# Block products for all input projections, and half of the output projection moved beside attention

## The chip, the core and the metric

The kernel runs on one core of a Trainium2 chip. TensorE (PE) multiplies matrices and adds up in 8 banks of PSUM; VectorE (DVE), ScalarE (ACT) and GpSimd (POOL) work element by element; SyncE (SP) issues DMA transfers between DRAM and the on-chip memory. Each engine runs its own instructions in their order and waits on semaphores for the others. The metric is the device time of one execution in microseconds; less is better.

## The reference

One layer of a decoder, 1024 tokens by 1024 features, all in f32:

```
h    = x @ w_in                # columns: pool 512 | q 512 | k 512 | v 512 | forget gate 8
pool = scale * GroupLinear(trailing_mean(u, win) - u)     # 4 groups of 128, win 2, 4, 8, 16
c    = cumsum(log_sigmoid(gate + b_f))                    # per head, 8 heads of 64
attn = softmax(q k' / 8 + c_t - c_s, causal) @ v
x    = layer_norm(alpha * x + concat(pool, attn) @ w_out)
x    = layer_norm(alpha * x + relu(x @ w_mlp1)**2 @ w_mlp2)   # hidden width 4096
```

## The kernel before

**Precision.** Each f32 operand is split into a rounded high part and the rest (`split`: a copy on ScalarE, L71, and a subtraction on VectorE, L72). A product is three matmuls: high by high, high by low, low by high (`three`, L83 to L85). So each 128-deep step of a product is three matmuls into a PSUM bank.

**Stages, in the order of time.**

1. Values and gate (L161 to L164): the 512 value columns and 8 gate columns, 260 in a matmul, for 8 tiles of 128 tokens by two halves by 8 depth steps by 3: 384 matmuls. The values (`V`) and all of x as high and low parts (`xs`, 8 blocks of the tag "B") stay on chip. Five blocks of the output weights are split meanwhile and put into DRAM (`split_output_weights`, L201).
2. Pool groups 3, 2 and 1 (`pool_group`), and keys and queries of head pair 0 (`qk_proj`): columns of 128 by two halves of 512 tokens by 8 depth steps by 3, 48 matmuls a column. The pooled differences pass through a small linear step (`pool_linear`) and into `mix_dram`.
3. Attention, head pairs 0 to 3. A unit is one head and 256 query rows. `att_probs` makes scores on PE (L370, L371), adds the gate row and finds the row maximum in one VectorE operation (L376), and exponentiates on ScalarE (L378). `att_values`, for the unit before, transposes the probabilities (L398), splits them (L399, L400) and multiplies by the values (L414). `fillstep` puts projection matmuls between them: keys and queries of the next pair, and pool group 0 during the last pair. The gate row of a head is 1024 sums of logarithms, spread to 128 partitions by a transfer from `ncf_dram` (L347); the first POOL or VectorE operation on a score needs it.
4. Output projection (from L771): per 128-token tile two halves of 512 columns, each 8 depth blocks by 3 matmuls (4 pooled, 4 from attention); then alpha * x added (L809), the norm on VectorE (`Norm.on_vector`), and the tile transposed for the MLP (`x1_transposed`).
5. The MLP, from 412 us to the end, already in seven block products of half size (`product`, L627, and combinations).

**What sets the order.** The program is written in the order in which each engine is to work; a scheduler keeps this order on each engine. Buffers are slots of a tag with a fixed count (14 "B" slots of 1 MB, 10 "Q", 9 "A" of half that); a transfer into a slot waits until the slot's last readers are done. All loads named here are issued by SP, one after the other: one that waits for its slot holds up all behind it. POOL issues some stores.

Of the kernel before, what the change touches and what calls it, by code (L numbers as in the profile page):

```python
# [32 lines left out]
EARLY, LATE = (3, 2, 1), (0,)  # L33
# [3 lines left out]
def trunk(ctx, tc, xT, xn, wuqk, wvf, bf, poolw, pscale, wout, g1, b1, w1, w2, g2, b2, out):  # L37
# [10 lines left out]
    NBUF = {"S": 3, "U": 2, "B": 14, "Q": 10, "A": 9}  # L48
    uid = [0]

    def slot(tag, shape, dt=F32R):
        uid[0] += 1
        return sb.tile([P] + list(shape), dt, tag=tag, bufs=NBUF[tag], name=f"{tag}{uid[0]}")

# [18 lines left out]

    def load_w(src):
        st = slot("S", [KT, P], F32)
        nc.sync.dma_start(st, src)
        w = slot("B", [2, KT, P])
        split(w[:, 0], w[:, 1], st)
        return w[:, 0], w[:, 1]
# [29 lines left out]
    ASIDE = 3  # L109
    wo_dram = dr.tile([KT - ASIDE, 2, P, D], F32, name="wo_dram")  # L110


    xs = {}

    def load_x(c, kp):
        st = slot("Q", [2, CH], F32)
        x = slot("B", [2, 2, CH])
        if c or kp:
            nc.sync.dma_start(st, xT[c, kp])
        for k in range(2):  # L120
            t = x[:, k]
            xs[c, 2 * kp + k] = t
            first = c == kp == k == 0
            for i, r in enumerate((slice(0, 256), slice(256, CH)) if first else (slice(0, CH),)):
                if c == kp == 0:
                    (nc.scalar if first and i == 0 else nc.sync).dma_start(st[:, k, r], xT[c, kp, :, k, r])
                split(t[:, 0, r], t[:, 1, r], st[:, k, r])
                yield

    wv = []  # L130

    def load_wvf(kp):
        st = slot("S", [2, 2 * VW], F32)
        hi, lo = slot("A", [2, 2 * VW]), slot("A", [2, 2 * VW])
        wv.append((hi, lo))
        if kp:
            nc.sync.dma_start(st, wvf[kp])
        for k in range(2):
            if kp == 0:
                nc.sync.dma_start(st[:, k], wvf[kp, :, k])  # L140
            for c in [slice(0, VW), slice(VW, 2 * VW)] if kp == 0 and k == 0 else [slice(0, 2 * VW)]:
                split(hi[:, k, c], lo[:, k, c], st[:, k, c])
                yield

    V = [None] * NT
    z = small([P, NT, NH], "z")

    def vf_mm(t, half, dst, k):
# [24 lines left out]
    for kp in range(4):  # L173

        gw, gx = load_wvf(kp), load_x(0, kp)
        for g in (gw, gx, gw, gx, gw, gx):
            next(g, None)
# [300 lines left out]
    att_values(*pend)  # L478

# [691 lines left out]
```

## Time and profile before

| | us |
|---|---|
| median of 3 runs | 1040.67 (1040.50 to 1040.82) |
| span of the profiled execution, first to last instruction | 1039.2 |
| values and gate | 5.2 to 53.6 |
| pool groups 3 to 1, pair 0 | 53.6 to 110.3 |
| attention | 110.3 to 322.5 |
| output projection | 323 to 412 |
| MLP | 412 to 1039.2 |

The profiled execution's own time is its span; the median of the runs is 1.5 us above it. The stage borders are the starts of the first matmuls of a stage's lines. Engine rows are read as busy time, instructions in parentheses; a matmul's duration there is longer than the distance to the next one, since they overlap, so the price of a matmul is read from packed stretches and not from its mean.

### The profile page before, as it was taken

The page shows a single profiled execution, that of the slowest core. Times are in us where ns is not written, and L with a number is a line of the kernel's source. Part 1 is how long each engine was busy: PE and PEld are TensorE (multiplying, and loading weights), DVE is VectorE, ACT ScalarE, POOL GpSimd, SP SyncE. Part 2 cuts the span into 40 slices and gives each one's busy share as a digit, 9 for nine tenths or more (in the row PEclk, how much of TensorE's full clock was granted, in tenths as well). Part 3 has the DMA queues.
Part 4 walks back from the last instruction along what each step waited for, and adds up shares of the span by engine and source line. Part 5 has one row for each costly group of instructions (what it writes and reads, how often), then busy time and mean ns, then how long its engine had stood idle before and what let it go on. Part 6 is the DMA issues. An engine that isn't in the chain of part 4 may idle for free.

```text
span 1039.2 us, 14092 instructions
## 1 busy us (share of the span) xinstructions
PE 1016.9 (98%) x4976; PEld 844.9 (81%) x4976; DVE 760.8 (73%) x1303; ACT 510.7 (49%) x820; POOL 142.7 (14%) x246
## 2 busy tenths in 40 slices
PE   9999999999989999999999999999999999999996
PEld 9988888878777888887888888888788888888884
DVE  4776678777786887988878778788875566566547
ACT  4623566666673321676766766768531221122152
POOL 0200112111000021113122122120100000000057
PEclk9999999999999999999999999999999999999998
DMA  9702211111376642139667566566999888878753
GB/s 358 274 27 87 98 52 52 34 50 54 101 250 207 195 148 102 62 134 349 266 240 276 215 262 263 227 231 221 346 308 305 283 264 281 271 228 271 242 186 121
DMA packets 114678, 206.29 MB, mean 199 GB/s; under 512 B 9576, under 2 KB 77992, under 8 KB 114608
## 3 DMA queue, kind: packets, MB, share of 16 engines
q1 hardware_dynamic: 96896, 141.82, 41.1%
q0 software_dynamic: 17280, 62.92, 15.6%
q8 instruction: 39, 0.64, 0.2%
q10 hardware_dynamic: 432, 0.66, 0.2%
q14 instruction: 31, 0.25, 0.1%
HBM read 132.42 MB, written 72.94 MB: 198 GB/s over the span
## 4 chain that ended last, share of the span: by engine, by line
PE 50%; issue 4%; DVE 3%; DMA 1%; POOL 1%; SPq 0%; ACT 0%; DVEq 0%; POOLq 0%
PE s L981 15%; PE pv L981 8%; PE s L627 8%; PE mm L627 6%; PE pt L627 6%; PE pv L627 4%; PE pt L981 2%; PE mm L981 2%; DMA hid_dram<-A 1%; DMA A<-hid_dram 1%; DVE B L72 1%; POOL hid_dram L752 0%; POOL A L620 0%; SPq L960 0%; DVE A L750 0%
## 5 line engine op out<-in xcount | busy, mean ns | idle before, releaser
L71 ACT CAST B<-S 128x1024 fp32r<-128x1024 f32 (+1 forms) x79 | 69.0, 885 | 168.8 <-DMA S<-in_w_dram 61.2
L627 PE MATMUL s<-B,Q 128*128 128x512 f32 x480 | 113.5, 389 | 0.2 <-ACT B L71 0.2
L627 PEld LDWEIGHTS s<-B,Q 128*128 128x128 f32 x480 | 90.0, 188 | 19.3 <-ACT B L71 0.6
L72 DVE TENSOR_TENSOR B<-S,B 128x1024 fp32r<-128x1024 f32 (+1 forms) x79 | 79.4, 1013 | 29.9 <-ACT B L71 29.8
L981 PE MATMUL s<-B,Q 128*128 128x512 f32 x390 | 94.8, 389 | 0.0
L71 ACT CAST Q<-S 128x1024 fp32r<-128x1024 f32 x52 | 54.7, 1052 | 64.0 <-PE s L627 17.0
L981 PEld LDWEIGHTS s<-B,Q 128*128 128x128 f32 x390 | 73.2, 188 | 15.6
L981 PE MATMUL s<-B,A 128*128 128x512 f32 x333 | 83.1, 394 | 1.2 <-DMA A<-hid_dram 1.2
L752 POOL DMA_DIRECT2D hid_dram<-A x90 | 48.3, 542 | 217.1 <-ACT A L749 174.7
L981 PEld LDWEIGHTS s<-B,A 128*128 128x128 f32 x333 | 62.4, 188 | 15.9 <-DMA A<-hid_dram 1.9
L72 DVE TENSOR_TENSOR Q<-S,Q 128x1024 fp32r<-128x1024 f32 x52 | 63.4, 1219 | 15.6 <-ACT Q L71 15.5
L627 PE MATMUL pt<-B,Q 128*128 128x512 f32 x300 | 71.6, 389 | 0.0
L627 PE MATMUL mm<-B,Q 128*128 128x512 f32 x300 | 71.6, 389 | 0.0
L414 PE MATMUL pv<-A,B 128*128 128x256 f32 x320 | 64.0, 299 | 3.0 <-DVE A L400 1.6
L627 PEld LDWEIGHTS mm<-B,Q 128*128 128x128 f32 x300 | 56.3, 188 | 11.7
L627 PEld LDWEIGHTS pt<-B,Q 128*128 128x128 f32 x300 | 56.3, 188 | 11.7
L414 PEld LDWEIGHTS pv<-A,B 128*128 128x128 f32 x320 | 49.6, 188 | 19.0 <-ACT A L399 8.8
L400 DVE TENSOR_TENSOR A<-pt,A 128x512 fp32r<-128x512 f32 (+1 forms) x80 | 49.2, 634 | 18.2 <-ACT A L399 17.7
L378 ACT ACTIVATE A<-A,nm 128x1024 f32<-128x1024 f32 (+7 forms) x64 | 49.8, 778 | 20.0 <-DVE nm L376 19.6
L750 DVE TENSOR_TENSOR A<-A,A 128x1024 f32<-128x1024 f32 x45 | 53.6, 1220 | 0.0
L399 ACT CAST A<-pt 128x512 fp32r<-128x512 f32 (+1 forms) x80 | 41.7, 540 | 18.5 <-PE pt L398 17.3
L981 PE MATMUL pv<-B,Q 128*128 128x512 f32 x204 | 50.3, 390 | 0.0
(407 smaller groups left out, 2309.7 us busy)
## 6 DMA issues: line engine op xcount, KB each, us to landing
hid_dram<-A POOLq DMA_DIRECT2D x105, 512.0 KB, 4.0
S<-in_w_dram SPq DMA_DIRECT2D x62, 512.0 KB, 3.7
Q<-hid_dram SPq DMA_DIRECT2D x101, 256.0 KB, 5.1
A<-hid_dram SPq DMA_DIRECT2D x79, 256.0 KB, 4.5
S<-in_wuqk_dram SPq DMA_DIRECT2D x12, 512.0 KB, 3.3
wo_dram<-Q POOLq DMA_DIRECT2D x10, 512.0 KB, 4.0
B<-wo_dram SPq DMA_DIRECT2D x10, 512.0 KB, 4.1
A<-ncf_dram SPq DMA_DIRECT2D x8, 512.0 KB, 3.9
```

The costliest lines, as they stand in the source:

```text
L71: nc.scalar.copy(hi, src)
L72: nc.vector.tensor_tensor(lo, src, hi.bitcast(F32), ALU.subtract)
L378: nc.scalar.activation(pt[:, :nk], pt[:, :nk], AF.Exp, bias=nm, scale=-1.0, accum_out=rsum[h][:, i : i + 1])
L399: nc.scalar.copy(tt[:, 0, ev], tp[:, ev])
L400: nc.vector.tensor_tensor(tt[:, 1, ev], tp[:, ev], tt[:, 0, ev].bitcast(F32), ALU.subtract)
L414: nc.tensor.matmul(ov, V[j][:, h].rearrange("p s d -> p (s d)"), tt[:, s, a:b], start=(j == 0 and s == 0), stop=(j == 2 * m + 1 and s == 1),)
L627: nc.tensor.matmul(dst, b[x][:, k], A[a][y][:, k], start=first and k == 0 and i == 0, stop=k == H - 1 and i == 2, skip_group_check=not first,)
L750: nc.vector.tensor_tensor(x, x, hi.bitcast(F32), ALU.subtract)
L752: nc.gpsimd.dma_start(hid_dram[self.u, :, i, AT[name] : AT[name] + 2 * CH], part.rearrange("p q n t -> p (q n t)"))
L981: nc.tensor.matmul(dst, h[:, p_], w[q_], start=first and u == self.us[0] and j == 0, stop=u == self.us[-1] and j == 2, skip_group_check=no ...
```

## The change

- **Block products.** With x and the weights cut into halves along both the contracted axis and the output axes, a product of 2x2 blocks is formed from seven block products of sums instead of eight. The values do this with halves of tokens by halves of columns (`v_product`, 7 x 48 = 336 matmuls of 260). Pool groups and keys/queries are taken two columns at a time, in six `Columns` (groups 3 and 2; 1 and 0; key and query of each pair), 7 products of 12 matmuls each: 504 of 512 columns, instead of 576. On chip are now seven blocks of x (A11, A12, A22 and four sums S1 to S4), high and low: all 14 "B" slots. Block sums are made by POOL and VectorE, combinations of products by ScalarE and VectorE.
- **All before attention.** Every projection, all four pool groups too, is finished before attention. Values go to `v_dram`, keys and queries (high and low, `kq_dram`), the pooled mix, already split (`pool_dram`), and all 8 blocks of the split output weights (`wo_dram`) to DRAM. Keys and queries, values and four blocks of the output weights are loaded back into "B" slots as the blocks of x are let go (`load_pair`, `load_values`, `load_output_weights`).
- **Memory in phases.** The "Q" and "A" memory is given anew to each phase ("v", "c", "t", "m": values, columns, attention, rest) with other tags; a new tile waits for the last user of the memory that it covers.
- **Pooled half beside attention.** `fillstep` now runs `pooled_output`: the pooled half of the output projection, 192 matmuls, with alpha * x added, into `xa_dram`.
- **After attention** the output projection has only the attention half (192 matmuls); the tile is read from `xa_dram`; the inverse row sums are multiplied in on POOL; norms of tiles 0 to 5 use `by_three` (ScalarE and four POOL operations, stores by SP) instead of `on_vector`; the transposes come two tiles later instead of one.

On SP, at the end of the projections and the start of attention, before (S holds projection weights, A of L347 a gate row):

```order
L248 DMA ncf_dram<-Q_825 8x1024
L76 DMA S_1201<-in_wuqk_dram 128x1024
L76 DMA S_1483<-in_wuqk_dram 128x1024
L347 DMA A_1132<-ncf_dram 128x1024
L303 DMA mix_dram<-A_1045 128x4x256
L76 DMA S_1785<-in_wuqk_dram 128x1024
L76 DMA S_2082<-in_wuqk_dram 128x1024
```

And now (B of L522 are keys and queries of a pair, of L534 output weights, G a gate row, M the pooled mix, x the input tile):

```order
L529 DMA B_1736<-v_dram 128x2x1024
L534 DMA B_1738<-wo_dram 128x2x1024
L534 DMA B_1739<-wo_dram 128x2x1024
L534 DMA B_1742<-wo_dram 128x2x1024
L534 DMA B_1743<-wo_dram 128x2x1024
L522 DMA B_1750<-kq_dram 64x2x1024 x2
L522 DMA B_1751<-kq_dram 64x2x1024 x2
L522 DMA B_1752<-kq_dram 64x2x1024 x2
L562 DMA G_1759<-ncf_dram 128x1024
L658 DMA M_1814<-pool_dram 128x1024
L658 DMA M_1815<-pool_dram 128x1024
L661 DMA x_1818<-in_xn_dram 128x1024
```

The first gate row stood among the loads of projection weights; now it stands behind every transfer into the "B" slots, the second pair's too.

On PE at the same place, before (the last projection, the first scores, the pooled linear step):

```order
L85 MATMUL pt_1099<-B_187,B_1063 128x512
L370 MATMUL s_1137<-Q_975,Q_976 128x512
L371 MATMUL s_1137<-Q_975,Q_977 128x512
L370 MATMUL s_1142<-Q_975,Q_976 128x512
L371 MATMUL s_1142<-Q_975,Q_977 128x512
L370 MATMUL s_1150<-Q_975,Q_976 128x512
L371 MATMUL s_1150<-Q_975,Q_977 128x512
L370 MATMUL s_1155<-Q_975,Q_976 128x384
L371 MATMUL s_1155<-Q_975,Q_977 128x384
L83 MATMUL pv_1167<-A_899,U_1163 128x512
```

And now (L123 is the last product of the last column; the names s are score banks, of which there are three):

```order
L123 MATMUL pt_1542<-B_572,w_1557 128x512 x4
L585 MATMUL s_1764<-B_1673,B_1674 128x512
L586 MATMUL s_1764<-B_1673,B_1675 128x512
L585 MATMUL s_1769<-B_1673,B_1674 128x512
L586 MATMUL s_1769<-B_1673,B_1675 128x512
L585 MATMUL s_1777<-B_1673,B_1674 128x512
L586 MATMUL s_1777<-B_1673,B_1675 128x512
L585 MATMUL s_1782<-B_1673,B_1674 128x384
L586 MATMUL s_1782<-B_1673,B_1675 128x384
```

The small linear step that stood behind four scores is gone from here; eight scores stand at the head, and the first filler matmul (L85 into a bank mm) behind them.

The diff, cut to its core:

```diff
+    def phase(name, bufs):
+        local.close()
+        stage.clear()
+        pool = local.enter_context(tc.tile_pool(name=name, bufs=1, reuse_waits="tile"))
+        stage.update((tag, (pool, n)) for tag, n in bufs.items())
...
+    def v_product(dst, a, b, first, by_row=False):
+        A_, B_ = X[a], wv[b]
+        for o in range(4 * H):
+            k, j = (o // 4, o % 4) if by_row else (o % H, o // H)
+            tok = slice(j * P, (j + 1) * P)
+            for n, (x, y) in enumerate(((0, 0), (0, 1), (1, 0))):
+                nc.tensor.matmul(
+                    dst[j][:, 0:VW], A_[x][:, k, tok], B_[y][:, k], start=first and k == 0 and n == 0,
...
+    split_wv("T4", t4)
+    v_product(vb1, "A22", "T4", False)
+    for j in range(4):
+        tt(cc0[:, j], vb2[j][:, 0:VW], cc0[:, j], sub)
+    for j in range(4):
+        v_out(j, 0, 0, u1[:, j])
...
+    phase("c", {"wf": 2, "w2": 1, "w14": 4, "w3": 2, "cc": 2, "k": 2, "q": 2, "d": 4})
...
+        def p5(self):
+            self.b2 = bank()
+            product(self.b2, self.v["T1"], X["S1"], True)
+            nc.scalar.copy(self.cc[:, 1], self.b2)
...
+        def store(self, n, i, w):
+            nc.gpsimd.dma_start(kq_dram[self.pair, n, i], w.bitcast(F32))
...
+    def load_pair(p):
+        ks, q1, q2 = (slot("B", [2, S]) for _ in range(3))
+        for n, w in enumerate((ks, q1, q2)):
+            for r in range(2):
+                src = kq_dram[p, n, r * (n == 0)].rearrange("(e r) t -> r e t", e=2)
+                nc.sync.dma_start(w[r * HD : (r + 1) * HD].bitcast(F32), src)
...
+        order = ((cur, "p1"), (prev, "p7"), (cur, "p2"), (prev, "p3"), (cur, "p6"), (prev, "p4"), (cur, "p5"))
+        if i == n:
+            load_pair(0)
...
+    load_values()
+    load_output_weights(0)
+    load_output_weights(1)
...
+    phase("t", {"G": 3, "P": 6, "tt": 4, "M": 4, "x": 2})
...
+    def pooled_output():
+        for m in range(4):
+            mh = [slot("M", [NG, 256]) for _ in range(2)]
+            for i, w in enumerate(mh):
+                nc.sync.dma_start(w.bitcast(F32), pool_dram[m, i])
...
+                    for k in range(NG):
+                        three(yp, (a[0][:, k], a[1][:, k]), (wo[k][0][:, cs], wo[k][1][:, cs]), k == 0, k == NG - 1)
+                        if k < NG - 1:
+                            yield
+                    nc.vector.scalar_tensor_tensor(xt[:, cs], xt[:, cs], ALPHA, yp, ALU.mult, ALU.add)
+                    yield
+                nc.gpsimd.dma_start(xa_dram[t], xt)
...
-        if n % 8 == 0:
-            if p + 1 < NPAIR:
-                gen, pieces, over = qk_proj(p + 1, "mm"), 4 * KT + 1, 28
-            else:
-                gen, pieces, over = last_fill(), (2 * KT + 2) * len(LATE), 14
-            fill.update(gen=gen, credit=0.0, rate=pieces / over)
+        if n % 8 == 0 and unit[0] + 1 < NPAIR:
+            load_pair(unit[0] + 1)
         prob = att_probs(*unit)
         if n + 1 < len(order):
             gate_row(2 * order[n + 1][0] + order[n + 1][1])
...
+        nc.gpsimd.tensor_tensor(mf, mf, rb, ALU.mult)
+        mh = slot("Q", [4, 256]), slot("Q", [4, 256])
+        split(*mh, mf)
...
+            if len(done) > 1:
+                x1_transposed(*done.pop(0))
             nm = Norm(xt, gam, bet, x1_dram[t])
             for i, c in enumerate(nm.cols):
-                nc.vector.scalar_tensor_tensor(xt[:, c], xt[:, c], ALPHA, yp[i], ALU.mult, ALU.add)
+                tt(xt[:, c], xt[:, c], yp[i], add)
                 nm.stats(i)
-            nm.on_vector()
+            if t < NT - 2:
+                nm.by_three()
+            else:
+                nm.on_vector()
```

More of the change, by code (lines that the diff above doesn't have):

```diff
@@ L52, in slot @@
         uid[0] += 1
[L53 removed]
+        pool, n = stage[tag] if tag in stage else (sb, NBUF[tag])
+        return pool.tile([P] + list(shape), dt, tag=tag, bufs=n, name=f"{tag}{uid[0]}")
     def small(shape, tag, dt=F32, bufs=1, pool=None):
@@ L130, in trunk @@
[L130 to L143, printed above, removed]
```

544 lines of the change are left out of this document (333 added, 211 removed).

## The prediction

> **What bounds the kernel now.** I read the page first: busy shares, slices, chain.
>
> ```profile
> span 1039.2 us, 14092 instructions
> PE 1016.9 (98%) x4976; PEld 844.9 (81%) x4976; DVE 760.8 (73%) x1303; ACT 510.7 (49%) x820; POOL 142.7 (14%) x246
> ...
> PE   9999999999989999999999999999999999999996
> ...
> PEclk9999999999999999999999999999999999999998
> ...
> PE 50%; issue 4%; DVE 3%; DMA 1%; POOL 1%; SPq 0%; ACT 0%; DVEq 0%; POOLq 0%
> ```
>
> PE is busy in every slice at a full granted clock, and the chain of waits names nothing of size beside it. So a matmul removed is worth what it takes, unless something else becomes late. Next I read stretches (columns: us, then busy us and instructions of PE, PEld, DVE, ACT, POOL, then PE clock, DMA share, GB/s).
>
> ```profile
> 8.00:28.00 20.00, 20.00 (x168) 19.95 (x168) 9.04 (x20) 8.57 (x16) 0.00 (x0) 1.00 1.02 406
> 520.00:620.00 100.00, 100.00 (x443) 82.81 (x442) 81.13 (x102) 67.64 (x86) 20.66 (x37) 1.00 0.64 247
> ...
> 5.20:53.60 48.40, 46.91 (x386) 46.66 (x386) 29.58 (x64) 24.34 (x46) 5.53 (x10) 1.00 0.81 320
> 53.60:110.30 56.70, 56.70 (x256) 46.77 (x255) 38.59 (x77) 16.93 (x27) 0.52 (x1) 1.00 0.20 68
> 110.30:322.50 212.20, 204.99 (x1201) 168.00 (x1200) 160.43 (x390) 137.83 (x301) 30.34 (x79) 1.00 0.28 93
> ```
>
> The first two rows are packed PE and give prices: 20.00/168 = 0.119 us for a 260-column matmul, 100/443 = 0.226 us for one of 512 columns. The last three are the stages that the change touches: values and gate (5.2 to 53.6 us), three pool groups and pair 0 (to 110.3), attention (to 322.5). In the first two PE hardly waits, and DMA has room in the second (share 0.20). Attention is looser: 212.2 us for the work costed below at 184.
>
> **Matmuls removed.** The value projection does 336 products of 260 columns instead of 384, the key, query and pool columns 504 of 512 instead of 576. 48 x 0.119 + 72 x 0.226 = 5.7 + 16.3 = **22.0 us** off PE. The MLP from 412 us is untouched.
>
> **Values and projections (+11).** Seven products need block sums and combinations, on VectorE mostly. The nearest rows:
>
> ```profile
> L72 DVE TENSOR_TENSOR B<-S,B 128x1024 fp32r<-128x1024 f32 x17 | 20.6, 1219 | 1.7 <-ACT B L71 1.7
> L162 DVE TENSOR_TENSOR B<-s,B 128x256 fp32r<-128x256 f32 x6 | 2.5, 422 | 12.2 <-ACT B L161 12.2
> L164 DVE TENSOR_TENSOR z<-s,bf 128x4 f32<-128x4 f32 x6 | 0.9, 153 | 0.0
> L569 POOL TENSOR_TENSOR Q<-Q,S 128x1024 f32<-128x1024 f32 x4 | 9.7, 2414 | 266.2 <-ACT Q L568 266.1
> mix_dram<-A SPq DMA_DIRECT2D x3, 512.0 KB, 2.9
> ```
>
> VectorE in the value stage: 14 splits of x blocks, 7 of weights and 4 sums at 1.22 us (30.5), 12 combinations of 260 columns at 0.42 (5.0), 16 outputs at 0.42 + 0.15 (9.2): 44.7 us, where PE needs 336 x 0.119 = 40.0. Unhindered, PE would end at 5.2 + 40 = 45.2. VectorE can't end before about 4 + 44.7 = 49, and POOL's 8 sums (19 us at 2.41) lie between its steps; I take the end at about 50, +5 (bounds 3 and 10). Then the first columns' weights go into memory that the value stage's tiles held, so their split waits for the last value outputs and the store of them to DRAM: 2.9 us to land, and some 1.5 for the outputs before: +4 (0, if the scheduler's next tile lies in free memory, to 8). Column work loads VectorE about as much as PE while weights are split, combined and rounded: +2 (0 to 4). Sum +11, bounds 3 and 22.
>
> **The start of attention (+25).** This is the largest term. Before, the gate row of the first head was fetched long ahead:
>
> ```profile
> 90.77 0.38 SPq L347 DMA_DIRECT2D A<-ncf_dram  x1
> ...
> 110.10 0.39 PE L85 MATMUL pt<-B,B 128*128 128x512 f32 x1
> 110.33 0.39 PE L370 MATMUL s<-Q,Q 128*128 128x512 f32 x1
> 110.98 0.69 DVE L376 CUSTOM_DVE_ANT_0 A<-s,A 128x512 f32<-128x512 f32 x1 [2.27 <-PE s L371]
> ```
>
> It was issued at 90.8 us, 20 us before the first scores; PE went from projection to scores without a gap. In the change SP's order puts ahead of this row (now L562): pair 0's keys and queries (6 transfers of 0.52 MB), the values (4 of 1.05), half the output weights (4 of 1.05), pair 1's keys and queries (6 of 0.52). That is 14.7 MB, and the row makes 15.2. All go into slots that the blocks of x hold until the last column's products have read them. Call T the end of the projections. A product is 12 x 0.226 = 2.7 us; nine follow the first release, so transfers start at about T - 25, the second half of the weights' slots come free at T - 4, and pair 1's last slots at T. SP issues in order, so the row can't be issued before T. What they bring:
>
> ```profile
> q1 hardware_dynamic: 96896, 141.82, 41.1%
> q0 software_dynamic: 17280, 62.92, 15.6%
> ...
> A<-ncf_dram SPq DMA_DIRECT2D x8, 512.0 KB, 3.9
> ```
>
> At a full DMA share (1.02, 8 to 28 us above) the chip moved 0.41 MB per us. SP's transfers share one queue (q1). POOL's queue (q0) stores the keys and queries of the last two pairs meanwhile: 8 x 0.52 = 4.2 MB. 19.4 MB / 0.41 = 47 us from T - 25: the row is there at about T + 22, with 2 us to land T + 24. PE fills its three score banks with 6 matmuls (1.4 us) and stops: the first softmax operation (L591) needs the row, and values, transposes and filler stand behind the scores on PE. Stopped 22.5 us, then about 3 us until transposes flow again (0.69 and 0.75 for the maxima, 1 for the exponential, 0.6 for a transpose's copy): +25. Bounds: 12, if POOL's stores don't slow SP's queue (15.2/0.41 = 37 us: T + 12) and start-up is short, and 31, if the queue runs at 0.36.
>
> The Trainium skill's page "DMA: Bandwidth & Descriptors", section Specifications, gives an HBM limit of about 358 GB/s per core. By it 19.4 MB would take 54 us and the term would be about 32; the row of 406 GB/s over 20 us contradicts it here, and the measurement decides.
>
> **Attention (-5).** Its own matmuls and VectorE's groups:
>
> ```profile
> L414 PE MATMUL pv<-A,B 128*128 128x256 f32 x320 | 64.0, 299 | 3.0 <-DVE A L400 1.6 <-ACT A L399 0.9
> ...
> L398 PE MATMUL pt<-ident,A 128*128 128x128 f32 x288 | 42.3, 273 | 1.1 <-DVE A L400 0.7 <-ACT row L433 0.3
> ...
> L370 PE MATMUL s<-Q,Q x96: 277/389/501, 110.3 to 305.9; 128*128 128x512 f32 x48, 128*128 128x256 f32 x32, 128*128 128x384 f32 x16
> ...
> L400 DVE TENSOR_TENSOR A<-pt,A 128x512 fp32r<-128x512 f32 (+1 forms) x80 | 49.2, 634 | 18.2 <-ACT A L399 17.7
> L376 DVE CUSTOM_DVE_ANT_0 A<-s,A 128x512 f32<-128x512 f32 (+3 forms) x64 | 37.3, 586 | 10.1 <-PE s L371 5.2 <-POOL A L363 3.7 <-issue 0.6
> L376 DVE CUSTOM_DVE_ANT_0 A<-s,A,nm 128x512 f32<-128x512 f32 (+3 forms) x32 | 17.5, 547 | 1.9 <-DVE nm L376 0.7 <-PE s L371 0.2 <-PE pt L398 0.2
> L420 DVE TENSOR_TENSOR U<-pv,U 64x256 f32<-64x256 f32 x32 | 13.5, 421 | 11.4 <-ACT U L419 11.0
> ...
> L376 DVE DVE_READ_ACCUMULATOR2_ANT nm<- 128x1 f32 x96 | 8.0, 83 | 0.0
> ...
> L809 DVE SCALAR_TENSOR_TENSOR A<-A,s 128x512 f32<-128x512 f32 x8 | 5.5, 682 | 3.7 <-PE s L85 2.6 <-DMA A<-in_xn_dram 1.1
> ```
>
> By columns, at 0.226 per 512: values 320 of 256 (36), transposes 288 of 128 at about 0.11 (31), scores, L371 like L370, 96 of 512, 64 of 256, 32 of 384 (35): about 103. Before, 354 filler matmuls made another 80, so 184, and the stage lost 28 of its 212 us. Now the filler is 192 matmuls: 43, so 147. If the loss keeps its proportion (15%) it is 22: the stage's loss falls by 5 or 6; I take -5. Bounds: VectorE now has 49.2 + 37.3 + 17.5 + 13.5 + 8.0 + 2.5 (reciprocals) = 128, and 16 additions of the filler at 0.68 (11): 139 us. If it can't go above the 0.76 busy share that it had (160.4/212.2), the stage takes 139/0.76 = 183, a loss of 36: +8. If it reaches 0.86, 162, a loss of 15: -13.
>
> **Output projection (+3).** PE has 192 matmuls here instead of 384, the other half being the filler just costed. Per tile PE has 24 x 0.226 and 8 transposes: 6.3 us. Six tiles' norms get four POOL operations of 128x512 each, and half an inverse-row product (1.2). The rows for such an operation lie far apart:
>
> ```profile
> L620 POOL TENSOR_TENSOR A<-A,Q 128x512 f32<-128x512 f32 x2 | 4.0, 2015 | 22.9 <-DVE Q L616 22.9
> ...
> L581 POOL TENSOR_TENSOR A<-A,S x2: 1257/1260/1264, 1029.5 to 1032.0; 128x512 f32<-128x512 f32 x2
> ```
>
> At 1.26 POOL needs 6.2 per tile, level with PE, and the transposes lag by two tiles: 0 to +3. At 2.02 it needs 9.3: 3 x 6 = 18 less the lag, +15. The same code elsewhere (L581) had 1.26, so I stay near it: +3.
>
> **Sum.** 1039.2 - 22.0 + 11 + 25 - 5 + 3 = 1051.2 in the profile's span; the median of the runs lies 1.5 above the span, so **1052.7 us**, slower by 12. No edit is costed at nothing; the extra stores of V, of the output weights and of the pooled part lie in the projections, where DMA's share was 0.20.
>
> **Rivals.** *A, faster: the gate row isn't late.* The break-even is the row landing 12 us sooner, at about T + 12. If the earlier transfers are through by T, because slots come free sooner than I read or the ring serves the row beside the others, only the 3 us of refilling are left: 1052.7 - 22 = **1031**. For it: one gate row is 0.5 MB, and 3.9 us to landing is usual. Against: SP issues in order, on one queue, and pair 1's slots come free only at T. *B, about even: only SP's own bytes count*, the stores give way; start 13 instead of 25: **1041**. For: no row here shows the one queue slowing the other. Against: the DMA share was 1.02 at 406 GB/s, so there is no room for both. *C, slower: POOL becomes the bound in the output projection*, 2.02 us an operation: 1052.7 + 12 = **1065**. For: L620's row; against: L581's. *D, slower: attention is held by VectorE's share*, 0.76: 1052.7 + 13 = **1066**. Against: that share is a mean over a stage in which VectorE waited for ScalarE (18.2 and 11.4 us in the groups above), not a limit. That the change doesn't do what it says is excluded: 336 and 504 matmuls stand in its order.
>
> The skill's page "SBUF — State Buffer", section "SBUF: two separate sides", says that VectorE with two SBUF inputs and POOL take turns at one port pair, each blocking the other for a whole instruction. It speaks for C, and L620's 2.02 beside L581's 1.26 fits it; it sets no number above.
>
> **How the numbers follow.** Forecast 0.55, A 0.13, B 0.12, C 0.10, D 0.10. The forecast's own bounds, taken together as independent (7, 13, 8 and 3 below, 11, 6, 13 and 12 above), give about 1036 to 1074. The range is 1034 to 1070: A falls out below, C and D are inside, and the rest is about 2 in 10. A difference of 0.2% (2 us) is about what a measurement here can tell from none. Faster: A, half of B, and 0.02 of the forecast's low end: 0.21. Same: 0.06. Slower: 0.73.
>
> **What would show it.** PE idle for some 22 us right after the last projection, released by the gate row's transfer, at about T + 24 with DMA at full share; PE's projections ending near 10 us past a sum without stalls; attention after the start about 169 us; 5 to 7 us per tile in the output projection. I am wrong if PE goes from projections to attention without a pause, if the value stage ends near 46 us, or if the output projection shows POOL busy all through.

## Result: 1161 us, slower by 11.6%

The changed kernel took 1161.14 us (median of 4 runs, 1158.04 to 1163.72) against 1040.74 us before: ratio 1.1155, 95% interval 1.1132 to 1.1178. The direction was forecast, the size was not: 1052.7 us was predicted, 1070 the upper end of the range.

The head of the changed kernel's page answers the rows that stand ahead of the prediction:

```profile
span 1160.1 us, 14216 instructions
...
PE 1046.2 (90%) x4856; PEld 844.6 (73%) x4856; DVE 795.7 (69%) x1296; ACT 535.0 (46%) x845; POOL 262.1 (23%) x344
...
PE   6787879736999998789999999999999999999995
...
PEclk9789789877999999799999999999999999999998
...
PE 67%; DMA 13%; DVE 9%; issue 5%; POOL 3%; ACT 2%; SPq 0%; DVEq 0%; POOLq 0%; ACTq 0%
```

120 matmuls fewer, as promised (4856 for 4976), and yet PE is busy 29 us longer; it idles in most of the first 18 slices, and the granted clock, at full throughout before, falls in most of the same slices. By stages (us, then busy us and instructions of PE, PEld, DVE, ACT, POOL, PE clock, DMA share, GB/s; values, columns, start of attention, attention, output projection, MLP):

```profile
5.20:69.70 64.50, 49.94 (x337) 48.00 (x336) 52.97 (x71) 29.82 (x51) 25.16 (x8) 0.84 0.45 161
69.70:239.20 169.50, 137.82 (x538) 106.41 (x537) 105.25 (x137) 58.43 (x81) 54.85 (x60) 0.88 0.60 215
239.20:275.10 35.90, 5.32 (x17) 3.77 (x16) 7.05 (x17) 4.67 (x8) 3.48 (x8) 0.59 1.03 368
275.10:442.60 167.50, 162.08 (x1008) 133.01 (x1006) 121.55 (x321) 104.21 (x250) 36.89 (x87) 1.00 0.63 183
442.60:511.40 68.80, 55.79 (x240) 44.21 (x241) 39.45 (x86) 28.78 (x46) 43.82 (x31) 0.88 0.49 147
511.40:1160.10 648.70, 631.20 (x2707) 505.23 (x2705) 468.08 (x662) 306.81 (x408) 96.30 (x128) 0.99 0.69 236
```

Beside the prediction's own sum, split by the same borders:

| stage | before | after | by the prediction | missed |
|---|---|---|---|---|
| values and gate | 48.4 | 64.5 | 45.0 (to 50.2 us) | 19.5 |
| projections by columns | 56.7, the rest in attention | 169.5 | 125.3 (528 x 0.226 + 6) | 44.2 |
| start of attention and attention | 212.2 | 203.4 | 194 (25 + 147 + 22) | 9.4 |
| output projection | 89.8 | 68.8 | 53.4 (8 x 6.3 + 3) | 15.4 |
| MLP, untouched | 626.9 | 648.7 | 626.9 | 21.8 |

The rows of PE's waits (us in total, times, longest) name the places before the MLP:

```profile
PE s L585 <- DVE nm L591: 30.6, 1, 30.6
PE mm L85 <- ACT q L80: 9.0, 1, 9.0
PE pt L123 <- ACT U L385: 7.2, 1, 7.2
PE pv L85 <- ACT q L80: 6.9, 1, 6.9
PE s L167 <- DVE A L243: 5.7, 1, 5.7
PE s L167 <- DVE B L81: 5.4, 3, 2.9
```

The first is the start of attention, the one loss that the prediction saw. The others, and the MLP, it did not see. The experiments take them one by one.

### The profile page after: what moved, and what is told of

Its sections match the earlier page's. It is cut to its first block, busy times and chain, and to the rows that moved or that the text cites. A ratio compares the mean times of both kernels' runs of the same rounds, so it can differ in the third digit from the quotient of the medians.

```text
span 1160.1 us, 14216 instructions
## 1 busy us (share of the span) xinstructions
PE 1046.2 (90%) x4856; PEld 844.6 (73%) x4856; DVE 795.7 (69%) x1296; ACT 535.0 (46%) x845; POOL 262.1 (23%) x344
## 4 chain that ended last, share of the span: by engine, by line
PE 67%; DMA 13%; DVE 9%; issue 5%; POOL 3%; ACT 2%; SPq 0%; DVEq 0%; POOLq 0%; ACTq 0%
PE s L1167 14%; PE s L123 10%; PE pv L1167 7%; PE pt L123 7%; PE mm L123 7%; PE pv L123 4%; PE pv L629 3%; PE pt L613 2%; PE pt L1167 2%; DMA G<-ncf_dram 2%; PE mm L1167 2%; DVE B L81 2%; PE s L585 1%; PE s L586 1%; DMA S<-in_w_dram 1%
## 5 line engine op out<-in xcount | busy, mean ns | idle before, releaser
L80 ACT CAST B<-S 128x1024 fp32r<-128x1024 f32 (+1 forms) x64 | 53.1, 842 | 168.1 <-PE s L1167 58.4
L123 PE MATMUL s<-B,Q 128*128 128x512 f32 x480 | 116.9, 395 | 0.1
L123 PEld LDWEIGHTS s<-B,Q 128*128 128x128 f32 x480 | 89.9, 188 | 22.7 <-ACT B L80 1.0
L1167 PE MATMUL s<-B,Q 128*128 128x512 f32 x390 | 97.1, 395 | 0.0
L81 DVE TENSOR_TENSOR B<-S,B 128x1024 fp32r<-128x1024 f32 (+1 forms) x64 | 61.1, 962 | 31.7 <-ACT B L80 31.5
L123 PE MATMUL pt<-B,Q 128*128 128x512 f32 x300 | 73.9, 395 | 0.1
L123 PE MATMUL mm<-B,Q 128*128 128x512 f32 x300 | 73.6, 395 | 0.0
L768 POOL TENSOR_TENSOR Q<-Q,S 128x1024 f32<-128x1024 f32 x4 | 9.6, 2402 | 272.6 <-ACT Q L767 272.5
L593 ACT ACTIVATE P<-P,nm 128x1024 f32<-128x1024 f32 (+7 forms) x64 | 49.7, 777 | 41.4 <-DVE nm L591 40.6
L629 PE MATMUL pv<-tt,B 128*128 128x256 f32 x320 | 65.8, 305 | 3.3 <-ACT tt L614 2.2
L123 PEld LDWEIGHTS pt<-B,Q 128*128 128x128 f32 x300 | 56.2, 188 | 14.3 <-DVE Q L81 0.6
L123 PEld LDWEIGHTS mm<-B,Q 128*128 128x128 f32 x300 | 56.3, 188 | 13.7
L615 DVE TENSOR_TENSOR tt<-pt,tt 128x512 fp32r<-128x512 f32 (+1 forms) x80 | 49.5, 635 | 21.7 <-ACT tt L614 21.2
L585 PE MATMUL s<-B,B 128*128 128x512 f32 (+2 forms) x96 | 36.2, 378 | 30.6 <-DVE nm L591 30.6
L629 PEld LDWEIGHTS pv<-tt,B 128*128 128x128 f32 x320 | 47.8, 189 | 21.1 <-ACT tt L614 11.6
L591 DVE CUSTOM_DVE_ANT_0 P<-s,G 128x512 f32<-128x512 f32 (+3 forms) x64 | 37.5, 586 | 32.4 <-DMA G<-ncf_dram 24.5
```

Of the source, the lines that this page charges most:

```text
L80: nc.scalar.copy(hi, src)
L81: nc.vector.tensor_tensor(lo, src, hi.bitcast(F32), ALU.subtract)
L123: nc.tensor.matmul(dst, b[x][:, k], a[y][:, k], start=first and k == 0 and i == 0, stop=k == H - 1 and i == 2, skip_group_check=not first,)
L585: nc.tensor.matmul(sp, Q1[:, qs], KS[:, a:b], start=True, stop=False)
L591: nc.vector.tensor_tensor_reduce(pt[:, a:b], sp[:, : b - a], nb[:, a:b], -1.0, top, ALU.add, ALU.min, nm)
L593: nc.scalar.activation(pt[:, :nk], pt[:, :nk], AF.Exp, bias=nm, scale=-1.0, accum_out=rsum[h][:, i : i + 1])
```

## Experiments

### An untouched MLP that is 22 us slower: addresses

The MLP's code is the same, its instructions too. Two 50 us stretches from the middle of its first and its second product, before and after:

```profile
600.00:650.00 50.00, 50.00 (x223) 41.38 (x222) 40.67 (x50) 33.63 (x42) 11.13 (x20) 1.00 0.67 257
900.00:950.00 50.00, 50.00 (x220) 41.08 (x219) 31.70 (x45) 11.26 (x15) 0.00 (x0) 1.00 0.83 262
```

```profile
600.00:650.00 50.00, 50.00 (x216) 40.24 (x215) 39.63 (x50) 33.95 (x44) 8.98 (x16) 1.00 0.65 240
900.00:950.00 50.00, 50.00 (x216) 40.20 (x215) 30.85 (x44) 10.83 (x14) 0.00 (x0) 1.00 0.88 285
```

PE is packed in all four at a granted clock of 1.00, and does 216 matmuls where it did 223 and 220. Between the first and last start of the first product's longest packed run (1114 matmuls before, 1187 after) a matmul takes 226.7 ns before and 233.2 ns after. Matmuls of 260 columns keep about 120 ns in both, and the MLP's first blocks, both operands in B slots, 227 to 228: so not a slower clock, which would slow all. What differs is where the operands lie: with the memory of the phases laid behind the other tiles, the MLP's Q and A slots now start at 128 modulo 256 bytes (the remainder of the address by 256) and B at 224; before, Q and B both started at 32, and the A slots at 32, 96, 160 and 224 in turn.

Theory: the two operands' distance in address costs. Rival: a lasting slow state after the idle stretches. Four layouts, each the same program with an unused small tile:

```diff
 # before_padB: B and U move by 32 bytes
         st = slot("Q", [2, CH], F32)
+        if c == kp == 0:
+            nc.vector.memset(small([P, 8], "pad"), 0.0)
         x = slot("B", [2, 2, CH])
...
 # before_all0: the same line ahead of the first Q slot; everything moves
...
 # after_pad: the same line ahead of the norm's rows; the memory of all phases moves by 32
...
 # before_B64: small([P, 16], "pad") in the place of before_padB; B moves by 64
```

> The kernel before with one unused 32-byte tile laid in front of the B slots: B and U move from an address of 32 modulo 64 to 0, everything else stays at 32. Same instructions, same order. Theory 'address' (the 233.3 ns instead of 226.7 ns between packed 512-column matmuls in the changed kernel come from the stationary and the moving operand lying at different remainders modulo 64): nearly all 512-column matmuls here pair B with Q or A, so they go to about 233 ns; some 3500 of them x 6.6 ns = 23 us, about 1060 to 1064 us in all. Rival 'clock' (the changed kernel's idle stretches leave TensorE in a slower state for the rest of the run): no change, 1040.7.

> The kernel before with the unused 32-byte tile in front of all slots: Q, S, A, B and U all move from 32 to 0 modulo 64. Theory 'address' in the form 'only a difference between the two operands costs': no change, 226.7 ns, 1040.7 us. In the form 'an operand at 0 (or at 32) costs by itself': the spacing of 512-column matmuls moves, to 233 ns (1060 us) if 0 is the bad one for the stationary operand, or below 226 ns if 32 is. Rival 'clock': no change.

> The changed kernel with the unused 32-byte tile ahead of the memory of its phases: Q, A and all phase slots move from 0 to 32 modulo 64, as B has. Theory 'address': spacing of 512-column matmuls back to 226.7 ns, 3300 x 6.6 ns = 22 us off, about 1138 us. Rival 'clock': 1161 and 233 ns stay, since the idle stretches stay.

Measured: before_padB 1057.13 us, ratio 1.0139 (1.0116 to 1.0162); before_all0 1040.59, ratio 0.9986 (0.9974 to 0.9998); after_pad 1147.90, 13 us less than the changed kernel. A pad of 32 bytes makes the unchanged kernel 15 us slower, with 216 matmuls in the stretch:

```profile
600.00:650.00 50.00, 50.00 (x216) 40.16 (x215) 37.58 (x47) 33.09 (x42) 10.04 (x18) 1.00 0.61 234
```

The rival falls. The 23 us expected were too many because pairs of B with B (pool groups, the MLP's first blocks) keep 227 to 228, and the second product's matmuls of B with A were at 230.6 before and go to 233.0 only. after_pad came to 229 ns only, not 226.7, so equality modulo 64 is not enough. I took 128 for the period, and tried to win by it: before the change every second A slot lay 64 off modulo 128, and the second MLP product ran at 228.8 ns on the mean.

```diff
 # before_a128: A slots of 4224 bytes instead of 4160, Q, A and B at one remainder modulo 128
-        hi, lo = slot("A", [2, 2 * VW]), slot("A", [2, 2 * VW])
+        if kp == 0:
+            nc.vector.memset(small([P, 16], "pad"), 0.0)
+        hi, lo = (slot("A", [2, 2 * VW + 8])[:, :, 0 : 2 * VW] for _ in range(2))
...
 # before_p256: A in memory of its own, 4160 bytes a slot in the value stage, 4096 after it
+    phase("v", {"A": 9})
...
+    phase("r", {"A": 9})
```

> The kernel before with A slots of 4224 bytes instead of 4160 and padded, so that Q, S, A and B all start at the same remainder modulo 128 (before, every second A slot was 64 off; room comes from one shared small tag, one small tile less of two kinds). Theory 'remainder modulo 128': the second MLP product's 512-column matmuls, 228.1 to 228.8 ns between packed starts, go to 226.7; some 1350 x 1.8 ns = 2.4 us off: about 1038.3, ratio 0.9977. Rival 'modulo 64 alone counts, the 228 come from the streamed loads': no change, ratio 1.000.

> The kernel before with the A slots in memory of their own (slots of 4160 bytes in the value stage, of 4096 after it) and two unused small tiles, so that Q, B and, after the value stage, every A slot start at 32 modulo 256; instructions and order otherwise the same. Theory 'remainder modulo 256' (226.7 ns where both operands agree modulo 256, more elsewhere; a layout that agreed modulo 128 but not 256 had 233.2): the second MLP product, whose A slots were at 224, 32, 96 and 160, goes from 228.5 to 226.7: 1350 x 1.8 ns = 2.4 us, about 1038.3, ratio 0.9977. Rival 'the 228.5 come from the streamed loads': 1040.7, ratio 1.000.

> The kernel before with an unused 64-byte tile ahead of the B slots: B at 96 modulo 256, Q at 32, A as before. Theory 'the cost depends on the distance modulo 256, small at 64': 229 ns between 512-column matmuls of B with Q (as in the changed kernel with 64 between them), 1046 to 1048 us. Rival 'any distance costs the full 6.6 ns': 233 ns, 1056.

before_a128: 1057.94 us, ratio 1.0154 (1.0140 to 1.0168). The theory in this form fell: Q lay at 0 and B at 128 modulo 256, and a distance of 128 costs as much as 32 or 96, 233.2 ns. before_B64, at 64: 229 ns, 1046.99 us, ratio 1.0057 (1.0036 to 1.0078). before_p256, with Q, B and all A slots at 32 modulo 256: 1039.11 us, ratio 0.9981 (0.9971 to 0.9991), and the second product at 226.7:

```profile
900.00:950.00 50.00, 50.00 (x223) 41.40 (x222) 31.99 (x47) 10.87 (x15) 0.00 (x0) 1.00 0.84 268
```

| distance of B's start from Q's, modulo 256 | 0 | 32 | 64 | 96 | 128 |
|---|---|---|---|---|---|
| ns between packed 512-column matmuls | 226.7 (four layouts, best5 below among them) | 233.2 | 229 (two layouts) | 233.2 | 233.2 |

So some 15 of the MLP's 22 us and some 3 in the columns are a matter of where the memory lies, shown from both sides. From the MLP's 100th 512-column matmul to its last, 592.3 us became 607.5; best5, with equal remainders, takes 590.7. It is not the full 6.5 ns for each of 2700, because the second product's A slots cost already before. Of the MLP's other 7 us, 4 lie in its first 100 matmuls, where VectorE is busy without a pause (28.0 of 28 us from 512 on), and 2.5 behind its last matmul; these were not followed further. What in the chip makes the distance cost, was not looked into. before_p256 is 0.19% faster than the kernel before, little more than its measurement can tell.

### The value stage: VectorE and POOL

Operations on VectorE in the value stage of the changed kernel (x, mean ns):

```profile
L81 DVE TENSOR_TENSOR B<-Q,B 128x1024 fp32r<-128x1024 f32 x12 | 21.7, 1828 | 1.9 <-ACT B L80 1.8
L250 DVE TENSOR_TENSOR Q<-Q,Q 128x1024 f32<-128x1024 f32 x2 | 5.8, 2946 | 0.0
```

and on POOL:

```profile
L269 POOL TENSOR_TENSOR Q<-Q,Q 128x1024 f32<-128x1024 f32 x2 | 6.6, 3340 | 0.0
```

The prediction costed the first at 1.22 us and POOL's at 2.41. Both are slower here, where the other works beside them; the next run takes POOL's share away.

```diff
 # after_vdve: the value stage's block sums
-    nc.gpsimd.tensor_tensor(t1, t1, wr["B12"], add)
+    tt(t1, t1, wr["B12"], add)
...
 # and so for t2, t3, t4 and the two loops over xr
```

> The changed kernel with the block sums of the value stage (six places, eight operations of 1024 or 1040 columns) on VectorE instead of POOL; nothing else. Theory 'the two engines hold each other up' (VectorE's operations of 1024 columns take 2.4 to 3.0 us between 20 and 46 us instead of 1.22, POOL's 3.4 instead of 2.4): VectorE's get back to 1.22 us, the value stage ends near 58 us instead of 70, and the kernel gains about 12 us, 1149. Rival 'VectorE has too much work in this stage anyway' (45 us, now 55): the stage ends at 66 us or later, gain under 5 us.

Measured 1151.18 us; the values end at 55.3 us instead of 69.7, and the same group is back at its price (the stage's row, then the group's):

```profile
5.20:55.30 50.10, 43.91 (x335) 42.53 (x333) 46.13 (x71) 29.56 (x51) 0.00 (x0) 0.93 0.45 160
...
L81 DVE TENSOR_TENSOR B<-Q,B 128x1024 fp32r<-128x1024 f32 x12 | 14.3, 1220 | 0.1
```

VectorE now has eight operations more and is busy 46.1 us instead of 53.0. The theory holds; 4 of the 14 us came back in the columns, which got 3 us longer, and at the start of attention. In the columns PE now waits 8.5 us for the first columns' weights, and ScalarE, which makes them, 7.0 us for a store of the values: the prediction's +4 for this place was right in kind (3.3 and 1.4 us of waits in the changed kernel).

### The columns: PE's order and the pooled differences

Waits of 9.0 and 6.9 us stand at the pooled linear step (L85, which needs the split difference q): its matmuls lie in PE's order right behind the product after which VectorE starts the windowed sums, some ten operations of 1.2 us for the two groups. The restart costs more on top. On PE's timeline (start, us, line) 11 packed matmuls ahead of the first wait, and 12 after it; then three stretches of the same place by engines:

```profile
106.63 2.73 PE L123 MATMUL mm<-B,w 128*128 128x512 f32 x11
...
123.06 5.49 PE L123 MATMUL mm<-B,w 128*128 128x512 f32 x12 [1.18 <-DVE q L469]
```

```profile
110.00:118.00 8.00, 0.00 (x0) 0.00 (x0) 7.90 (x14) 1.04 (x2) 0.00 (x0) 0.64 0.23 74
118.00:121.50 3.50, 2.91 (x6) 1.66 (x6) 3.46 (x6) 0.31 (x2) 0.00 (x0) 0.50 0.06 19
121.50:130.00 8.50, 6.65 (x16) 4.48 (x16) 4.42 (x8) 3.90 (x6) 2.81 (x4) 0.54 0.84 280
```

After 8 us without a matmul the granted clock is 0.5, and 12 matmuls take 5.5 us, where 12 packed ones take 3.0. Added up over the trace, PE was busy at a granted clock of 0.5 for 15 us in the values, 25 in the columns, 10 in the output projection and 5 around the start of attention; half of these 55 us, some 27, is the price of the slow restarts. Before the change PE had no busy time at half clock in any stage. The Trainium skill's page "TensorE: Matmul & The Clock Gate", section "Part 1: The HAM clock gate (the "warmup" mystery)", says that PE drops to half its clock after an idle window of about 3.4 us and is busy for about that time before it comes back. The rows agree with the half; by it, each long stall of the forecast would have had a price of its own behind it. With the way back they do not agree: PE was busy for 9.6 of the 12 us from 118.0 to 130.0, with gaps of at most 1.2 us, and the last row still has 0.54.

```diff
 # after_lin: difference and linear step of each group in places of their own (x.pool() returns the four steps)
...
-            at(i + 1, 6, x.pool)
+            for (ii, pl), f in zip(((i + 1, 6), (i + 2, 1), (i + 2, 1), (i + 2, 3)), x.pool()):
+                at(ii, pl, f)
```

> The changed kernel with the pooled differences and the linear step of each group set apart by one or more block products, and the second group of a column behind the first, instead of both groups in one place; same operations. Theory 'PE waits in its order for the pooled differences' (9.0 and 6.9 us at 109 and 147 us, each with a slow restart): both waits go, some 16 us of idle and 8 of slow restart, about 1138. Rival 'the slots of the q tag are what is late' (a store has to land before the next difference can be written): the waits move behind the later linear steps and the gain is under 8 us.

Measured 1147.99 us, 13 less. In the columns both waits go: 138.9 us instead of 169.5, PE's idle part falls from 30 to 7 us. 16 of these 23 are the two waits. 7 are the third row of the waits above, which this edit does not touch: the copy U (L385) stood on ScalarE behind a key operation that waited 12.4 us for the store of the keys that lay in its slot before. Why that wait is gone too was not tested. The remaining 8 us are slow restart (busy time at half clock falls from 25 to 9 us). But the start of attention grows from 35.9 to 52.5 us, its wait from 30.6 to 47.0 (the two stages, then the wait):

```profile
69.60:208.50 138.90, 130.58 (x538) 102.40 (x537) 101.32 (x137) 58.09 (x81) 53.81 (x60) 0.96 0.63 224
208.50:261.00 52.50, 5.50 (x18) 3.98 (x17) 7.27 (x17) 4.87 (x8) 3.69 (x8) 0.56 1.03 356
...
PE s L586 <- DVE nm L592: 47.0, 1, 47.0
```

So the theory holds for the two waits, and more than half of the gain is given back at once: the end of the projections came 31 us sooner, the loads that attention waits for only 14.

### The start of attention: two waits, one behind the other

```diff
 # after_gate1: the phase's memory and the first gate row ahead of the other loads
+    phase("t", {"G": 3, "P": 6, "tt": 4, "M": 4, "x": 2})
...
+    gate_row(0)
     load_values()
     load_output_weights(0)
...
 # after_gateact: the same, and the first row on ScalarE's queue
+            (nc.sync if h else nc.scalar).dma_start(gate_rows[h], ncf_dram[h : h + 1, :].to_broadcast([P, S]))
...
 # after_gate3: as after_gate1, the second pair's loads at unit 4, the filler from unit 3 on
```

> The changed kernel with the first gate row's transfer issued ahead of the values, the output weights and the second pair; nothing else moved. Theory 'start of attention waits for the gate row alone': the 30.7 us wait of the scores for L591 falls to a few us, about 1133 us. Rival 'the next transfer in the same queue is late too' (the filler's first matmul stands behind eight scores on PE and needs output weights, the pooled mix and the input tile, which come behind the second pair): the wait moves from the scores to the first filler matmul, gain 0 to 8 us, 1153 to 1161 us.

> The changed kernel with the first gate row issued by ScalarE on its own queue instead of SP's; nothing else than in the run with the row ahead of the values. Theory 'the row waits for what stands before it in SP's queue': on a queue of its own it lands within 5 us of its issue although the DMA engines are full; the wait at the first scores goes from 30.7 to under 15 us, and the first filler matmul, which needs the pooled mix behind the second pair, waits next. Rival 'all queues wait for the same bytes': it lands as late as in SP's queue, wait 17 us or more.

> The changed kernel with the first gate row ahead of the values, the second pair's keys and queries asked for four units later, and the filler starting with the fourth unit instead of the first. Theory 'queue' (the gate row waits for what stands ahead of it on SP and for the bytes of both queues): 17 us of wait were left with the row alone moved; with 3.1 MB less around it, about 8 us less: a wait near 9 us and 1140. Rival 'stores of POOL's queue hold it': the wait stays at 15 us or more, 1147.

Measured: after_gate1 1148.4 us (one execution), the wait 17.2; after_gateact 1146.3 (one execution), 17.5; after_gate3 1160.9, 17.4. In the changed kernel the row was issued at 249.2 us and landed at 270.4, at full DMA share. With the row ahead of most loads, 13 us are gained, more than the rival allowed, and not nearly the whole. In after_gateact the row lands in 7 us from a queue of its own, with the DMA engines as full, and yet the first softmax operation starts at 254.9 us: what the theory says of the row holds, and the wait is as long as the rival's, for another reason:

```profile
240.01 0.33 ACTq L557 DMA_DIRECT2D G<-ncf_dram  x1
...
247.29 0.42 POOL L579 TENSOR_TENSOR G<-G,maskb 128x128 f32<-128x128 f32 x1 [3.11 <-DMA G<-ncf_dram]
...
254.87 0.69 DVE L592 CUSTOM_DVE_ANT_0 P<-s,G 128x512 f32<-128x512 f32 x1 [11.95 <-DMA kq_dram<-k]
```

The releaser is no longer the row but a store: the output tile P of the first softmax lies in memory that a key tile of the last pair held, and that tile's store to DRAM, issued at 243 us on POOL's queue, lands at 254.6. The two waits lay in parallel; the row's, in SP's queue, was the longer, and behind it stood the store's. In the changed kernel that store landed at 257.4 us, 13 before the row, and 13 us are what moving the row gained. So the place in SP's queue decides when the row comes (7 us on a queue of its own, 21 on SP's), and the store of the key tile decides the rest; this is after_gate3's rival, and its theory of the queue fell. That the store takes 11.5 us because the DMA engines are full is likely and was not shown apart. Whether a P tile in other memory takes the 17 us away was not tried. after_gate3 gave its gain back: the filler came late, and from its first to its last value matmul attention took 181 us, in after_gate1 167.

Two runs were to shorten the transfers, on top of after_lin:

```diff
 # after_lin_kq: one layout in DRAM, so that a load fills 128 partitions
+            for r in (i,) if n == 0 else (0, 1):
+                for e in range(2):
+                    nc.gpsimd.dma_start(kq_dram[self.pair, n, e, r * HD : (r + 1) * HD], w[e * HD : (e + 1) * HD].bitcast(F32))
...
+            nc.sync.dma_start(w.bitcast(F32), kq_dram[p, n].rearrange("e q t -> q e t"))
...
 # after_lin_wo: output weights split in columns 0 to 3 instead of 2 to 5
-        at(2 + k // 2, 1 + 3 * (k % 2), lambda k=k: split_output_weights(k))
+        at(k // 2, 1 + 3 * (k % 2), lambda k=k: split_output_weights(k))
```

> The kernel with the linear steps set apart (after_lin, 47.0 us of wait at the first scores), and in addition keys and queries laid out in DRAM so that each load fills 128 partitions in one transfer instead of 64 in each of two; the queries are stored twice for it, 1 MB more per pair. Theory 'transfers into 64 partitions run at half the rate' (in after_lin 240 to 250 us moved 220 GB/s at a DMA share of 1.04, where 416 to 421 were moved 20 us before): 6.3 MB of loads take 15 us instead of 29, less 5 us of additional stores: the wait falls by about 10 us to 37, and no stretch of full share is below 380 GB/s. Rival 'the dip is DRAM, not the partitions': rates and wait stay, or the wait grows by 5 us with the stores.

> The kernel with the linear steps set apart, and in addition the splitting of the output weights two columns earlier: 4.2 MB of loads and 8.4 MB of stores move from the last four columns into the first four. Theory 'bytes set the landing of the first gate row' (DMA is at full share from about 170 us on): about 6 MB less in the last 60 us are 15 us, the wait falls from 47 to about 32 us. Rival 'the place in SP's order and the slots set it': the wait stays at 45 to 48 us.

Both were misses in time: 1153.7 us each, in one execution each, some 4 to 6 more than after_lin. In the first the rate is as expected. A stretch of after_lin, and one of after_lin_kq:

```profile
240.00:250.00 10.00, 0.00 (x0) 0.00 (x0) 0.00 (x0) 0.00 (x0) 0.00 (x0) 0.50 1.04 220
```

```profile
240.00:250.00 10.00, 0.00 (x0) 0.00 (x0) 0.00 (x0) 0.00 (x0) 1.07 (x2) 0.50 1.03 420
```

Loads into 64 partitions move 220 GB/s at a full share, into 128 partitions 420; the Trainium skill's page "SBUF — State Buffer", section "Door 1: The DMA port swizzle", tells it so (64 partitions reach half the ports, about 218 GB/s), and the rows agree. But PE now waits 16 us for the keys and queries of pair 0 ahead of the wait for the row (33.1 us), with twice the stores of queries before them; the two were not taken apart further. In the second the wait fell to 41.6 us, while the columns got 11 us longer; with the splits among the pooled sums, a wait of 6.6 us for the pooled difference is back. Neither made attention start earlier: its first value matmul stands at 264.0 us in after_lin and at 270.4 and 270.5 here.

### The output projection

```diff
 # after_outvec
-            if t < NT - 2:
-                nm.by_three()
-            else:
-                nm.on_vector()
+            nm.on_vector()
...
-        nc.gpsimd.tensor_tensor(mf, mf, rb, ALU.mult)
+        tt(mf, mf, rb, ALU.mult)
```

> The changed kernel with the norms of all tiles and the inverse row sums on VectorE, as before the change; nothing else. Theory 'POOL's own order holds the transposes up' (7.3 and 1.9 us of waits for L781; the first norm's POOL operations stand behind a product that waits for its rows): the output projection goes from 69 to about 57 us, 1149. Rival 'the loads are late, not POOL': 66 us or more remain, 1158 or more.

Measured 1158.99 us. In the changed kernel PE waits 11.1 us in this stage for POOL (rows of the changed kernel):

```profile
PE s L799 <- POOL B L781: 7.7, 2, 7.3
PE pt L799 <- POOL B L781: 3.4, 2, 1.9
```

POOL's operations of 512 columns took 1.26 to 1.31 us, nearly the lower of the two prices, but for two of the 24 at 2.15. What was late is their order: the first norm's stand behind a product (L971) that waits until 463.4 us for the inverse rows. On VectorE the stage takes 62.5 us instead of 68.8, where the theory had 57: the transposes now wait 6.6 us for the norm's last VectorE operation. And 6 us return in the MLP's first blocks (654.6 us instead of 648.7): a half-confirmed cause, and no gain in sum.

### All corrections at once

```diff
 # best5: after_vdve, after_outvec, after_lin, after_lin_kq and after_lin_wo together, and
+    nc.vector.memset(small([P, 24], "pad"), 0.0)
...
+    phase("t", {"g": 1, "m": 2, "G": 2, "P": 6, "tt": 4, "M": 2, "x": 2})
...
+    gate_row(0)
+    load_mixed(0)
     load_values()
...
+        if n % 8 == (3 if n < 8 else 0) and unit[0] + 1 < NPAIR:
+        if n == 2:
+            fill["rate"] = 64 / 106
```

> All corrections at once: phase memory at the remainder of the B slots modulo 128, the value stage's sums and all norms on VectorE, linear steps set apart, 128-partition loads of keys and queries, output weights split two columns earlier, the first gate row issued by ScalarE's queue ahead of the values, the first pooled mix in memory that comes free early, the filler from the third unit on. Theory (each loss has the cause named): values end near 54 us, columns take 125, start of attention 12, attention 170, output projection 60, MLP 627: about 1050. Rival 'bytes remain the bound at the start of attention': a wait of 25 us or more there, 1070 or more.

Measured 1120.19 us (two runs), ratio 1.0755 (1.0719 to 1.0792): 41 us better than the change, 79 worse than before. The rival's case (from the last columns to the first units of attention):

```profile
202.00:253.80 51.80, 20.16 (x73) 15.82 (x74) 9.18 (x17) 6.40 (x11) 11.14 (x22) 0.66 1.03 414
```

```profile
PE mm L85 <- DMA m<-pool_dram: 28.1, 1, 28.1
```

Now the first filler matmul waits 28 us for the pooled mix, behind the output weights and the second pair (it was written ahead of them; the scheduler put it behind, probably because its slot comes free late), with the DMA engines at 414 GB/s for the whole of 52 us. The key tile's store holds here too: VectorE's first softmax operation waits 17.7 us for it, to 241.7 us, and PE's wait ends at 251.1. 22 us of PE time cannot pay for it.

## Why the prediction was wrong, point by point

- **Matmuls removed (22.0 us)**: right in count. Right in price for the layout before; the new layout raised the price of most 512-column matmuls by up to 6.5 ns, also of those in the MLP, which the change does not touch. The sentence "The MLP from 412 us is untouched" is one step that failed: 21.8 us instead of nothing, some 15 of them addresses.
- **Values and projections (+11, bounds 3 and 22)**: the step that failed most, by 64 us. For the values the work was listed rightly and priced from rows in which the other engine was idle; with POOL and VectorE together the group took 1.83 us instead of 1.22 (14 us by after_vdve). For the columns "Column work loads VectorE about as much as PE", +2, was an average where the order decides: PE stood behind the pooled differences (16 us) and behind a store of keys (7), and the slow restarts behind these waits cost 8, together the 31 us of after_lin. That the extra stores are covered by a DMA share of 0.20 was read from the kernel before; in the new columns it was 0.60, and a store was waited for. (In the bounds, the lower end of 3 lies 8 below 11, not 7; it moves the range's low end by less than 1 us.)
- **Start of attention (+25, bounds 12 and 31)**: right in place and in what PE waited for, too small in size: the wait was 30.6 us against 22.5, the row landed 31 us after the last product against 24, and the stage took 35.9 us, above the bound of 31. Mis-sized was the rate of the 64-partition loads (220 GB/s, not 410). Not seen was the store that stands behind the row: "only the 3 us of refilling are left" without the row is wrong, 17 were left.
- **Attention (-5)**: right in size, 167.5 us after the start, 169 by the sum; no run tests the share by which the loss was scaled.
- **Output projection (+3, upper bound 15)**: mis-sized, 18 measured, with some 5 of slow restart and addresses among it. In the main not the price of a POOL operation, as rival C had it, but POOL's order, and that only in part: on VectorE 6 us of it go, and return in the MLP.
- **Rivals**: A and B had the row early; even where it is early (after_gateact) PE waits 17 us. D did not happen. The Trainium skill's rule that VectorE and POOL take turns (page "SBUF — State Buffer", section "SBUF: two separate sides"), which the prediction set beside C, fits the value stage, where it was not applied: 1.83 us beside POOL, 1.22 without.
- **The range** took the terms as independent. They were not: each long stall also lowers the clock of what follows it, and each was bounded by rows of a kernel in which PE never stalled.

## What to carry to other kernels

Before trusting that untouched code keeps its time, compare the operands' addresses modulo 256 and the distance between packed matmuls in both traces; a small unused tile cost 1.4% here (before_padB). Price an operation of VectorE or POOL from a stretch in which the other engine does what it will do beside it, and look for the first PE instruction in the new order whose operand is not ready, not for the average load of a stage. Where everything is loaded at one border, a stall removed ahead of it comes back as a wait for the transfers.

## What was not expected of the hardware

- A 512-column matmul with the stationary operand in one slot and the moving one in another takes 226.7 ns where both start at the same remainder modulo 256, 229 at a distance of 64, 233.2 at 32, 96 and 128. 260-column matmuls stayed at about 120 ns; their A slots lay at several distances in every layout, so for them no distance was tested alone.
- After a stall of 9 us the granted clock is 0.5, and a dozen matmuls behind it take 5.5 us instead of 3.0; such restarts cost some 27 us before the MLP, beside 95 us of plain waiting.
- Operations of 1024 columns on VectorE took 1.83 us on the mean and up to 3.0 while POOL worked, 1.22 without; POOL's 3.3 instead of 2.4.
